# Turning the strips of the two output projections through tiles of the ring

## The chip, the cores and the metric

The kernel runs on one core of one Trainium2 chip. The metric is the device time of one execution in microseconds (us); lower is better. Times given for a kernel are medians over executions on the chip; the profile is one more execution, recorded by the hardware profiler.

## What is computed

The reference is a two-layer decoder trunk on 256 tokens of width 2048 in float32. Cut to what matters here:

```
for i in range(DEPTH):                                  # DEPTH = 2
    h = rms_norm(x, attn_norm_w[i])
    x = x + mixer(h, ...)                               # attention, then "@ w_o": the output projection
    x = x + conv_ffn(rms_norm(x, ffn_norm_w[i]), ffn_w_up[i], ..., ffn_w_down[i])
    gate = sigmoid(rms_norm(x, ple_norm_w[i]) @ ple_w_gate[i])
    x = x + gate * (p[i] @ ple_w_proj[i])
return rms_norm(x, final_norm_w)
```

The output projection multiplies the attention's result (256 x 2048 in layer 0, 256 x 1536 in layer 1) by `w_o` and adds the product to the stream x. The feed-forward part (FFN) then needs x, normalized, as the left operand of its up-projection.

## The kernel before

Every large product is made of float32 matmuls in a split form: each operand is a high part (`hi`, the value rounded to the matmul's type) and a low part (`lo`, the rest), and a block of 128 rows takes three matmuls for each half of the tokens (lines 360 to 362, `add_block`). ScalarE (ACT) makes `whi` of a raw weight tile (line 323) and VectorE (DVE) makes `wlo` (line 324); four pairs of `whi` and `wlo` exist (`NWSP = 4`), each holding two blocks of 128 rows, so that a pair is worth 12 matmuls of a strip. A product's output is made in strips of 512 columns, with tokens on the partitions, 128 tokens in each of two halves.

The next product wants x the other way round, with columns of x on the partitions. So each finished strip s of x is turned: DVE turns 32 x 32 squares of both halves into two tiles `y` (`turn_out`, line 248), a DMA on the queue of GpSimd (POOL) writes each `y` to a tile `there` in DRAM (line 251), and four DMAs read `there` back into a tile `turned` in the right order (`turn_in`, line 260). Then `use` makes four tiles `h` of it (`split_x`, lines 148 on ACT and 149 on DVE): the blocks 4s to 4s+3 of the next product's left operand. Below, h(s) stands for these four tiles of strip s, and y(s) for its two transposes.

`add_strips` runs a projection: for each of four strips it adds the product to x (line 983), squares it for the norm (line 216), and calls `Turned.add`, which first writes down the `use` of the strip ahead, h(s-1), and then the turning of strip s. The last strip's `use` is returned as `late` and is called by the next product. The calls to `add_strips` that make `h` are the output projection of each layer (`base` is 0) and the second half of each down-projection (`base` is not 0); the per-layer-embedding part (`ple`) has a `Turned` of its own.

The tiles `y` of these strips come from the pool `tmp`, under the tags `eh` and `el`, with one buffer each. The tiles `h`, the attention's results `o` and others come from the pool `ring`, with 42 buffers under one tag. The order of instructions on each engine is set ahead of time by a scheduler from the written order, the priorities, `issue_after`, and when tiles of a pool can be had; on the chip each engine then runs its list in order.

After the output projection the FFN takes its first two up-strips together (`products` with `side` 2 and `late`): both run over the blocks of h(0) to h(2), and then over those of h(3). In layer 1 the tiles are called `accv_12249` and `accv_12256` (the two halves of the gate strip), `accv_12353` and `accv_12360` (of the value strip), `h_11978` to `h_11987` for h(0), `h_12042` to `h_12051` for h(1), `h_12177` to `h_12186` for h(2) and `h_12461` to `h_12470` for h(3).

Of the kernel before, what the change touches and what calls it, by code (L numbers as in the profile page):

```python
# [80 lines left out]
def tile_trunk(ctx, tc, head_d, xT_d, x_d, pT_d, pos_d, vec_d, cst_d, csb_d, wqkv, wo_a, wkv, wq_b, wo_b, wup, wdn, wpg, wpp, gfin_d, out_d):  # L81
# [11 lines left out]
    def nm(s):  # L93
        uid[0] += 1
        return f"{s}_{uid[0]}"
# [7 lines left out]
    def rt(s, shape=(P, 512), dt=F32):  # L103
        return ring.tile(list(shape), dt, tag="kb", name=nm(s))

    def tt(s, shape=(P, S), dt=F32, tag=None, bufs=None):
        kw = {} if bufs is None else {"bufs": bufs}
        return tmp.tile(list(shape), dt, tag=tag or s, name=nm(s), **kw)
# [33 lines left out]
    def split_x(src, j, bases):  # L142

        out = []
        for b in bases:
            h = rt("h", dt=F32R)
            high, low = like(h[:, :S], src), like(h[:, S:], src)
            last["split"] = nc.scalar.activation(high, src, AF.Copy, scale=gain(b, j)).ins
            nc.vector.scalar_tensor_tensor(low, src, gain(b, j), f32(high), op0=OP.mult, op1=OP.subtract)
            out.append(h)  # L150
        return out
# [6 lines left out]
    def strip_of(t, s):  # L158
        return x[t][:, s * 512 : (s + 1) * 512]

    def load_table():

        table = nc.scalar.preload_act_table_set("natural_log_exp_and_others")
        tc.keep_in_program_order(table)
        return table
# [11 lines left out]
    class FirstNorm:  # L177


        def __init__(self):  # L180
            self.two = rt("first")
            self.s = self.two[:, :S]
            self.n = 0
            self.table = load_table()

        def add(self, src):

            if self.n == 0:
                nc.scalar.activation(self.two, src, AF.Square)
            else:  # L190
                q = tt("sq", (P, 768), tag="w", bufs=4)[:, :512]
                nc.scalar.activation(q, src, AF.Square)
                nc.vector.tensor_tensor(self.two, self.two, q, op=OP.add)
            self.n += 1
# [44 lines left out]
    def four(s):  # L239

        return tt(s, (P, 4 * S), tag="four", bufs=3)

    def turn_out(strips, ringed=False):

        there = dram.tile([2 * P, 512], F32, tag="turn", name=nm("there"))
        for t, strip in enumerate(strips):
            y = rt("y") if ringed else tt("y", (P, 768), tag=("eh", "el")[t], bufs=1)[:, :512]
            last["turned"] = nc.vector.transpose(  # L248
                y.rearrange("p (b o r) -> p o b r", b=4, o=4), strip.rearrange("p (o b c) -> p o b c", o=4, b=4)
            ).ins  # L250
            nc.gpsimd.dma_start(there[t * P : (t + 1) * P], y)  # L251
        return there

    def turn_in(there, ahead=0):

        z = four("turned").rearrange("p (a o r) -> p a o r", a=8, o=4)
        back = there.rearrange("(a c) (b f) -> b c a f", c=32, b=4)
        with tc.high_priority(offset=ahead) if ahead else ExitStack():
            for b in range(4):
                nc.gpsimd.dma_start(z[32 * b : 32 * b + 32].rearrange("p a o r -> p a (o r)"), back[b])  # L260
        return z

    def turn(s):
        z = turn_in(turn_out([strip_of(t, s) for t in range(2)]))
        return [z[:, :, o] for o in range(4)]

    class Turned:


        def __init__(self, use):  # L270
            self.use = use
            self.strip = None

        def add(self, s, later=False):
            if self.strip is not None:
                self.turn_strips(self.strip, later)
            self.strip = (s, turn(s))

        def turn_strips(self, strip, later):
            def use():  # L280
                with tc.issue_after(last["square"]), tc.issue_after(last["added"]):
                    self.use(*strip)

            self.waiting = use
            if not later:
                use()

        def late(self):
            self.use(*self.strip)

        def begin(self, tiles):
            return {4: self.waiting}

    def weights(W, s, n, fine=False, before=lambda k0: None, block=None, base=0, ringed=0):

# [81 lines left out]
    def products(jobs, xs, late=None, at=0, then={}, side=2, first=None, seven=None, plan=PLAN, host=lambda: None):  # L377
# [7 lines left out]
        if late is not None:  # L385
# [7 lines left out]
            def before(k0):  # L393
                if k0 + skip == at:
                    add()
                if k0 in then:
                    then[k0]()
# [24 lines left out]
            if at is None:  # L422
                W, s, base = jobs[0]
                ready = list(weights(W, s, 4, base=base + n))
                add()
# [36 lines left out]
    class Seven:  # L462
# [99 lines left out]
        def go_on(self):  # L562
            xs, n = self.xs[4:], len(self.xs) - 4
            ps = self.banks()[0]
            it = weights(self.W, self.strips[0], n, base=self.base + 4)

            def add(tiles, o):
                for k0, hi, lo in tiles:
                    for i in range(2):
                        add_block(ps[o], xs[k0 + i], o, hi[i], lo[i], False, k0 + i == n - 1, True)  # L570

            self.fifth()
            tiles = [next(it) for _ in range(2)]
            add(tiles, 0)
            self.sixth()
            add(tiles, 1)
            for k, o, hi, lo in (g for group in steps(hooked(it, {1: self.seventh}), n, 2) for g in group):
                add_block(ps[o], xs[k], o, hi, lo, False, k == n - 1, True)
            return ps
# [380 lines left out]
    def add_strips(W, xs, gain_of, norm, base=0, late=None, at=6, side=2, first=None, seven=None, plan=PLAN, host=None):  # L960

        out = []

        def use(s, blocks):
            for o, b in enumerate(blocks):
                out.extend(split_x(b, 4 * s + o, [gain_of]))

        turned = Turned(use)
        begun = [None]

        def hosted():
            if host is not None:
                begun[0] = host(out)
            if seven and norm is not None and not base:
                return turned
            return begun[0]

        jobs = [(W, s, base) for s in range(4)]
        for s, ps in enumerate(products(jobs, xs, late, at, {}, side, first, seven, plan, hosted)):
            if norm is not None and s == 3:  # L980
                norm.table = load_table()
            for t in range(2):
                last["added"] = nc.vector.tensor_tensor(strip_of(t, s), ps[t], strip_of(t, s), op=OP.add).ins
                if norm is not None:
                    norm.add(s, t)
            if norm is not None:
                turned.add(s, seven and not base and s == 2)
        return out, turned.late, begun[0]

    def ffn(i, xs, late, rc, began):  # L990
# [79 lines left out]
        def down_strips(gs, base, late, first, gain_of=None, norm=None):  # L1070
            if first:
                seven = Seven(wdn[i], 2, 3, gs, first.sums, base, ("acc", "two", "acc", "two"))
            else:
                seven = Seven(wdn[i], 2, 3, gs, block_sums(gs[:4]), base)
            return add_strips(wdn[i], gs, gain_of, norm, base, late, first=first, seven=seven)
# [93 lines left out]
    norm = FirstNorm()  # L1169
# [39 lines left out]
    for i in range(2):  # L1209
        norm = Norm()  # L1210
        seven = None
        host = lambda h: Seven(wup[i], 0, FB // 4, h, block_sums(h[:4]), 0, ("att", "acc", "acc", "acc"))
        h, late, began = add_strips(
            wo_a if i == 0 else wo_b,
            o,
            G_FFN + i * KB,
            norm,
            late=o_late,
            at=(10, 4)[i],
            side=2 + i,  # L1220
            seven=seven,
            plan=PLAN_WO,
            host=host if False else None,
        )
        rc = norm.done()
        pb = p_blocks(i)
        h, late, norm = ffn(i, h, late, rc, began)
        rc = norm.done()
        norm = Norm()
        if i == 0:  # L1230
            hq, xT, late = ple(i, h, late, pb, rc, norm, G_ATTN + KB)
            o, o_late = mixer_b(hq, late, lambda js: [split_x(xT[j], j, [G_KV])[0] for j in js], norm.done)
        else:
            ple(i, h, late, pb, rc, norm)
# [81 lines left out]
```

## Time and profile before

| | before |
|---|---|
| median of 3 runs | 2276.11 us (2276.03 to 2281.66) |
| the profiled execution's own time | 2277.94 us |
| its span in the trace | 2276.2 us |
| granted TensorE clock, mean | 0.999 |
| output projection of layer 0, last strip added to x | 374.5 us into the span |
| output projection of layer 1, last strip added to x | 1456.9 and 1460.5 us into the span |

The span is the trace from the first to the last instruction; 1.74 us of the execution's own time lie around it. The profiled execution is 1.83 us above the median of the runs. In the rows of a timeline the columns are: start, duration (both in us), engine, line, operation, output<-input, shape and count; in brackets the idle time of the engine ahead of the row and what ended it. A row with x2 or x4 merges neighbours.

### The profile page before, as it was taken

What the parts mean: (1) busy time and instruction counts of PE and PEld (TensorE: products, weight loads), DVE (VectorE), ACT (ScalarE), POOL (GpSimd) and SP (SyncE); (2) the same over time, 40 slices, a digit from 0 to 9 for tenths busy, and PEclk for the clock granted to TensorE, in tenths of its full rate; (3) what the DMA queues carried; (4) which work ended last, traced back from release to release, by engine and by line L of the source; (5) the groups of instructions that cost most, each with busy time, mean ns of one, the idle gap of its engine ahead of it and who ended that gap; (6) DMA issues with size and microseconds to landing.
All of it is one profiled execution on the core that took longest, in us unless ns stands there. A gap on an engine that the chain in (4) does not pass through costs nothing.

```text
span 2276.2 us, 28094 instructions
## 1 busy us (share of the span) xinstructions
PE 2262.8 (99%) x10095; PEld 1875.1 (82%) x10095; DVE 1720.8 (76%) x2532; ACT 1334.3 (59%) x1785; POOL 328.7 (14%) x575
## 2 busy tenths in 40 slices
PE   9999999999999999999999999999999999999998
PEld 7888888888888888888888888888888888888887
DVE  7778766788975888876787765768887588887665
ACT  6555555666644666655675554666664466665554
POOL 0211211111100111101021331211110011110100
PEclk9999999999999999999999999999999999999999
DMA  8678767686755867758587786868675577775863
GB/s 298 236 243 274 248 217 259 211 266 233 251 203 185 274 224 242 268 180 272 185 294 244 248 265 216 264 214 272 227 256 196 200 254 232 243 264 186 276 220 121
DMA packets 149549, 538.45 MB, mean 237 GB/s; under 512 B 16672, under 2 KB 17568, under 8 KB 149152
## 3 DMA queue, kind: packets, MB, share of 16 engines
q1 hardware_dynamic: 114560, 435.46, 55.0%
q0 software_dynamic: 32560, 95.98, 14.1%
q10 hardware_dynamic: 2288, 5.21, 0.7%
q8 instruction: 79, 1.29, 0.2%
q14 instruction: 62, 0.51, 0.1%
HBM read 486.52 MB, written 50.07 MB: 236 GB/s over the span
## 4 chain that ended last, share of the span: by engine, by line
PE 99%; DMA 1%; ACT 0%; DVE 0%; POOL 0%; issue 0%
PE accv L360 20%; PE accv L361 20%; PE accv L362 20%; PE seven L362 5%; PE seven L361 5%; PE seven L360 5%; PE seven L499 5%; PE two L362 4%; PE two L361 4%; PE two L360 4%; PE two L499 3%; PE two L626 1%; DMA turned<-there 0%; PE keys L626 0%; DMA vec<-in_head 0%; ACT whi L323 0%
## 5 line engine op out<-in xcount | busy, mean ns | idle before, releaser
L324 DVE TENSOR_TENSOR wlo<-raw,whi 128x1024 fp32r<-128x1024 f32 (+1 forms) x756 | 915.7, 1214 | 412.3 <-ACT whi L323 409.8
L323 ACT ACTIVATE whi<-raw 128x1024 fp32r<-128x1024 f32 (+1 forms) x756 | 794.8, 1053 | 654.6 <-PE accv L362 339.3
L360 PE MATMUL accv<-whi,h 128*128 128x512 f32 (+1 forms) x1496 | 580.9, 388 | 2.2 <-ACT whi L323 1.4
L362 PE MATMUL accv<-whi,h 128*128 128x512 f32 (+1 forms) x1496 | 580.8, 388 | 0.0
L361 PE MATMUL accv<-wlo,h 128*128 128x512 f32 (+1 forms) x1496 | 580.7, 388 | 0.0
L360 PEld LDWEIGHTS accv<-whi,h 128*128 128x128 f32 x1496 | 280.9, 188 | 60.7 <-ACT whi L323 2.0
L361 PEld LDWEIGHTS accv<-wlo,h 128*128 128x128 f32 x1496 | 280.9, 188 | 58.4 <-DVE wlo L324 0.7
L362 PEld LDWEIGHTS accv<-whi,h 128*128 128x128 f32 x1496 | 281.0, 188 | 57.4
L251 POOL DMA_DIRECT2D there<-y x162 | 91.7, 567 | 1265.4 <-DVE y L248 1245.5
L260 POOL DMA_DIRECT2D turned<-there x324 | 190.2, 594 | 453.7 <-DMA there<-y 195.6
L489 ACT ACTIVATE whi<-raw 128x1024 fp32r<-128x1024 f32 x119 | 126.0, 1059 | 103.5 <-PE accv L362 79.3
L490 DVE TENSOR_TENSOR wlo<-raw,whi 128x1024 fp32r<-128x1024 f32 x119 | 145.1, 1219 | 44.1 <-ACT whi L489 43.5
L362 PE MATMUL seven<-whi,h 128*128 128x512 f32 x384 | 150.0, 391 | 0.0
L361 PE MATMUL seven<-wlo,h 128*128 128x512 f32 x384 | 149.4, 389 | 0.0
L360 PE MATMUL seven<-whi,h 128*128 128x512 f32 x384 | 149.4, 389 | 0.0
L360 PE MATMUL accv<-whi,g 128*128 128x512 f32 x352 | 136.9, 389 | 0.0
L361 PE MATMUL accv<-wlo,g 128*128 128x512 f32 x352 | 136.9, 389 | 0.0
L362 PE MATMUL accv<-whi,g 128*128 128x512 f32 x352 | 136.9, 389 | 0.0
L360 PE MATMUL two<-whi,h 128*128 128x512 f32 x240 | 93.4, 389 | 0.0
L361 PE MATMUL two<-wlo,h 128*128 128x512 f32 x240 | 93.4, 389 | 0.0
L362 PE MATMUL two<-whi,h 128*128 128x512 f32 x240 | 93.4, 389 | 0.0
L248 DVE STREAM_TRANSPOSE y<-u 128x512 f32<-128x512 f32 x122 | 84.0, 699 | 5.0 <-DMA there<-y 4.6
(230 smaller groups left out, 3214.7 us busy)
## 6 DMA issues: line engine op xcount, KB each, us to landing
raw<-in_wup SPq DMA_DIRECT2D x176, 1024.0 KB, 5.5
raw<-in_wdn SPq DMA_DIRECT2D x88, 1024.0 KB, 5.4
there<-y POOLq DMA_DIRECT2D x171, 256.0 KB, 5.1
turned<-there POOLq DMA_DIRECT2D x324, 128.0 KB, 5.1
raw<-in_wqkv SPq DMA_DIRECT2D x40, 1024.0 KB, 5.5
raw<-in_wpg SPq DMA_DIRECT2D x32, 1024.0 KB, 5.5
raw<-in_wkv SPq DMA_DIRECT2D x24, 1024.0 KB, 5.5
raw<-in_wo_a SPq DMA_DIRECT2D x16, 1024.0 KB, 5.9
```

The lines of the kernel that those rows point to most:

```text
L248: last["turned"] = nc.vector.transpose(y.rearrange("p (b o r) -> p o b r", b=4, o=4), strip.rearrange("p (o b c) -> p o b c", o=4, b=4)).ins
L251: nc.gpsimd.dma_start(there[t * P : (t + 1) * P], y)
L260: nc.gpsimd.dma_start(z[32 * b : 32 * b + 32].rearrange("p a o r -> p a (o r)"), back[b])
L323: last["high"] = nc.scalar.activation(hi[:, c], r, AF.Copy).ins
L324: last["low weights"] = nc.vector.tensor_tensor(lo[:, c], r, f32(hi[:, c]), op=OP.subtract).ins
L360: nc.tensor.matmul(ps, xl, hi, start=first, stop=False, skip_group_check=again)
L361: nc.tensor.matmul(ps, xh, lo, start=False, stop=False, skip_group_check=again)
L362: nc.tensor.matmul(ps, xh, hi, start=False, stop=final, skip_group_check=again)
L489: last["high"] = nc.scalar.activation(hi, r, AF.Copy).ins
L490: last["low weights"] = nc.vector.tensor_tensor(lo, r, f32(hi), op=OP.subtract).ins
L499: nc.tensor.matmul(ps, x, y, start=begins, stop=ends, skip_group_check=True)
L626: run.append(nc.tensor.matmul(*args, skip_group_check=True, **kw).ins)
```

## The change

`turn` and `Turned` get an argument `ringed`, which reaches `turn_out`: with it the two `y` of a strip are tiles of the ring, and not the two single tiles of the tags `eh` and `el`. `add_strips` sets it where `base` is 0, so for both output projections: 4 strips x 2 halves x 2 layers, 16 tiles. The down-projections and `ple` keep the single tiles. The other lines removed belong to a delayed call of `use` (`later`, `turn_strips`, `begin`) whose condition holds in no call of this kernel: `seven` with `norm` and without `base` occurs nowhere.

```
-    def turn(s):
-        z = turn_in(turn_out([strip_of(t, s) for t in range(2)]))
+    def turn(s, ringed=False):
+        z = turn_in(turn_out([strip_of(t, s) for t in range(2)], ringed))
         return [z[:, :, o] for o in range(4)]
 
     class Turned:
-        def __init__(self, use):
+        def __init__(self, use, ringed=False):
             self.use = use
             self.strip = None
-
-        def add(self, s, later=False):
+            self.ringed = ringed
+
+        def add(self, s):
             if self.strip is not None:
-                self.turn_strips(self.strip, later)
-            self.strip = (s, turn(s))
...
                 with tc.issue_after(last["square"]), tc.issue_after(last["added"]):
-                    self.use(*strip)
...
+                    self.use(*self.strip)
+            self.strip = (s, turn(s, self.ringed))
...
-        turned = Turned(use)
+        turned = Turned(use, not base)
...
-            if seven and norm is not None and not base:
-                return turned
...
-                turned.add(s, seven and not base and s == 2)
+                turned.add(s)
```

The numbers and kinds of instructions stay the same on every engine; the order changes on PE, DVE and ACT, around the two output projections only. POOL and the queue of SP keep theirs. Line numbers after the class fall by 10 to 12 (324 becomes 314, 983 becomes 971).

On DVE, output projection of layer 1, strip 1 (its sums are `x_76<-accv_11741` and `x_77<-accv_11748`, its transposes `y_11991` and `y_11994`). Before:

```order
L983 TENSOR_TENSOR x_76<-accv_11741,x_76 128x512
L983 TENSOR_TENSOR x_77<-accv_11748,x_77 128x512
L248 STREAM_TRANSPOSE y_11991<-x_76 128x4x4x32
L324 TENSOR_TENSOR wlo_12087<-raw_12066,whi_12086 128x1024
L248 STREAM_TRANSPOSE y_11994<-x_77 128x4x4x32
L324 TENSOR_TENSOR wlo_12105<-raw_12102,whi_12104 128x1024
L983 TENSOR_TENSOR x_76<-two_11805,x_76 128x512
L983 TENSOR_TENSOR x_77<-two_11805,x_77 128x512
L324 TENSOR_TENSOR wlo_12121<-raw_12102,whi_12120 128x1024
L324 TENSOR_TENSOR wlo_12139<-raw_12136,whi_12138 128x1024
L149 SCALAR_TENSOR_TENSOR h_11978<-turned_11933,vec,h_11978 128x256
```

The same place on DVE with the change:

```order
L971 TENSOR_TENSOR x_76<-two_11805,x_76 128x512
L971 TENSOR_TENSOR x_77<-two_11805,x_77 128x512
L314 TENSOR_TENSOR wlo_12121<-raw_12102,whi_12120 128x1024
L314 TENSOR_TENSOR wlo_12139<-raw_12136,whi_12138 128x1024
L149 SCALAR_TENSOR_TENSOR h_11978<-turned_11933,vec,h_11978 128x256
L149 SCALAR_TENSOR_TENSOR h_11981<-turned_11933,vec,h_11981 128x256
L149 SCALAR_TENSOR_TENSOR h_11984<-turned_11933,vec,h_11984 128x256
L149 SCALAR_TENSOR_TENSOR h_11987<-turned_11933,vec,h_11987 128x256
L248 STREAM_TRANSPOSE y_11991<-x_76 128x4x4x32
L314 TENSOR_TENSOR wlo_12155<-raw_12136,whi_12154 128x1024
L248 STREAM_TRANSPOSE y_11994<-x_77 128x4x4x32
```

The transposes y(1) moved from right behind strip 1's sums to behind the four h(0), where y(2) stood before.

On DVE, the same projection, strip 3 (`y_12190`, `y_12193`) and h(2). Before:

```order
L983 TENSOR_TENSOR x_77<-accv_12079,x_77 128x512
L248 STREAM_TRANSPOSE y_12190<-x_76 128x4x4x32
L248 STREAM_TRANSPOSE y_12193<-x_77 128x4x4x32
L324 TENSOR_TENSOR wlo_12316<-raw_12313,whi_12315 128x1024
L235 TENSOR_REDUCE rcol_12201<-ssum_11664 128x2
L169 TENSOR_SCALAR rcol_12201<-rcol_12201 128x2
L324 TENSOR_TENSOR wlo_12332<-raw_12313,whi_12331 128x1024
L149 SCALAR_TENSOR_TENSOR h_12177<-turned_12061,vec,h_12177 128x256
L149 SCALAR_TENSOR_TENSOR h_12180<-turned_12061,vec,h_12180 128x256
L149 SCALAR_TENSOR_TENSOR h_12183<-turned_12061,vec,h_12183 128x256
L149 SCALAR_TENSOR_TENSOR h_12186<-turned_12061,vec,h_12186 128x256
```

With the change:

```order
L314 TENSOR_TENSOR wlo_12420<-raw_12417,whi_12419 128x1024
L149 SCALAR_TENSOR_TENSOR h_12177<-turned_12061,vec,h_12177 128x256
L149 SCALAR_TENSOR_TENSOR h_12180<-turned_12061,vec,h_12180 128x256
L149 SCALAR_TENSOR_TENSOR h_12183<-turned_12061,vec,h_12183 128x256
L149 SCALAR_TENSOR_TENSOR h_12186<-turned_12061,vec,h_12186 128x256
L248 STREAM_TRANSPOSE y_12190<-x_76 128x4x4x32
L314 TENSOR_TENSOR wlo_12436<-raw_12417,whi_12435 128x1024
L248 STREAM_TRANSPOSE y_12193<-x_77 128x4x4x32
```

The transposes y(3), which stood ahead of h(2), now stand behind it; between h(1) and h(2) y(2) moved in the same way, and in layer 0 all three.

On PE, where the FFN of layer 1 has used up h(1) (`h_12051` is its last tile). Before:

```order
L360 MATMUL accv_12256<-whi_12297,h_12051 128x512
L361 MATMUL accv_12256<-wlo_12298,h_12051 128x512
L362 MATMUL accv_12256<-whi_12297,h_12051 128x512
L360 MATMUL accv_12249<-whi_12315,h_12177 128x512
L361 MATMUL accv_12249<-wlo_12316,h_12177 128x512
L362 MATMUL accv_12249<-whi_12315,h_12177 128x512
```

With the change:

```order
L350 MATMUL accv_12256<-whi_12297,h_12051 128x512
L351 MATMUL accv_12256<-wlo_12298,h_12051 128x512
L352 MATMUL accv_12256<-whi_12297,h_12051 128x512
L350 MATMUL accv_12353<-whi_12349,h_11978 128x512
L351 MATMUL accv_12353<-wlo_12350,h_11978 128x512
L352 MATMUL accv_12353<-whi_12349,h_11978 128x512
```

Here 48 matmuls of the value strip over h(0) and h(1) moved ahead of the gate strip's 24 over h(2). In layer 0 PE keeps its order.

More of the change, by code (lines that the diff above doesn't have):

```diff
@@ L261, in turn_in @@
         return z
-    def turn(s):
-        z = turn_in(turn_out([strip_of(t, s) for t in range(2)]))
+    def turn(s, ringed=False):
+        z = turn_in(turn_out([strip_of(t, s) for t in range(2)], ringed))
         return [z[:, :, o] for o in range(4)]
     class Turned:
-        def __init__(self, use):
+        def __init__(self, use, ringed=False):
             self.use = use
             self.strip = None
-        def add(self, s, later=False):
+            self.ringed = ringed
+        def add(self, s):
             if self.strip is not None:
-                self.turn_strips(self.strip, later)
-            self.strip = (s, turn(s))
-        def turn_strips(self, strip, later):
-            def use():
                 with tc.issue_after(last["square"]), tc.issue_after(last["added"]):
-                    self.use(*strip)
-            self.waiting = use
-            if not later:
-                use()
+                    self.use(*self.strip)
+            self.strip = (s, turn(s, self.ringed))
         def late(self):
             self.use(*self.strip)
-        def begin(self, tiles):
-            return {4: self.waiting}
     def weights(W, s, n, fine=False, before=lambda k0: None, block=None, base=0, ringed=0):
```

## The prediction

> **What bounds the kernel now.** I read the page's table of engines first, then the chain of waits of TensorE (PE), then the same stretch engine by engine.
>
> ```profile
> span 2276.2 us, 28094 instructions
> PE 2262.8 (99%) x10095; PEld 1875.1 (82%) x10095; DVE 1720.8 (76%) x2532; ACT 1334.3 (59%) x1785; POOL 328.7 (14%) x575
> ```
>
> PE is busy all but 13.4 us of the span, so the time is that of its list of matmuls plus its idle time. Its waits on other engines:
>
> ```profile
> PE accv L360 <- ACT whi L323: 1.4, 1, 1.4
> PE warm L130 <- DVE zero L127: 1.2, 1, 1.2
> PE accv L360 <- DVE h L149: 0.9, 1, 0.9
> ```
>
> The first two are the program's start. The third is the only wait in the middle, and it is the change's place: the FFN of layer 1 waits for h(2). PE's rows around it, with the first matmul on an h:
>
> ```profile
> 1457.78 0.39 PE L360 MATMUL accv<-whi,h 128*128 128x512 f32 x1
> ...
> 1468.43 0.39 PE L362 MATMUL accv<-whi,h 128*128 128x512 f32 x1
> 1469.67 0.50 PE L360 MATMUL accv<-whi,h 128*128 128x512 f32 x1 [0.85 <-DVE h L149]
> ```
>
> The second row is the 48th matmul: (1468.43 - 1457.78) / 47 = 0.2266 us each. So 24 matmuls, one h(s) in one up-strip, are worth 5.44 us, and a pair of weights 2.72 us. Without a wait h(2) would have begun at 1468.66, so PE lost 1.0 us. That is about all that the change can win on PE; anything else it can only lose.
>
> **What the old tiles cost, and what stands in its place.** DVE in that stretch:
>
> ```profile
> 1436.93 0.70 DVE L248 STREAM_TRANSPOSE y<-x 128x512 f32<-128x512 f32 x1
> ...
> 1439.61 0.71 DVE L248 STREAM_TRANSPOSE y<-x 128x512 f32<-128x512 f32 x1 [0.87 <-DMA there<-y]
> ...
> 1446.90 1.69 DVE L149 SCALAR_TENSOR_TENSOR h<-turned,vec,h 128x256 fp32r<-128x256 f32 x4 [0.21 <-ACT h L148]
> 1448.51 0.70 DVE L248 STREAM_TRANSPOSE y<-x 128x512 f32<-128x512 f32 x1
> ...
> 1450.24 0.70 DVE L248 STREAM_TRANSPOSE y<-x 128x512 f32<-128x512 f32 x1
> ...
> 1461.11 1.30 DVE L248 STREAM_TRANSPOSE y<-x 128x512 f32<-128x512 f32 x2
> ```
>
> y(1) waited 0.87 us for the buffer `el`, on an engine with slack; removing that wait is worth nothing by itself. But look at when the transposes ran: y(1) at 1436.93, y(2) at 1448.51, y(3) at 1461.11, each as soon as sums and buffers allowed, so that several strips were on their way through DRAM together. In the new order of DVE y(s) stands behind all four h(s-1), and h(s-1) waits for the read-back of strip s-1. A ring gives its tiles in written order, in which `use` of strip s-1 comes first; that is how I read the order, but only the order itself enters the sum. On an engine that runs its list in order, three strips that overlapped become a serial chain: y(1), trip through DRAM, h(1), y(2), trip, h(2), y(3), trip, h(3).
>
> **One trip, from rows.** POOL (writes L251, read-backs L260) and ACT's first step on what landed:
>
> ```profile
> 1434.22 0.56 POOL L251 DMA_DIRECT2D there<-y  x1 [1.15 <-DVE y L248]
> 1440.07 2.35 POOL L260 DMA_DIRECT2D turned<-there  x4 [5.29 <-ACT whi L323]
> 1442.41 1.12 POOL L251 DMA_DIRECT2D there<-y  x2
> 1448.00 2.35 POOL L260 DMA_DIRECT2D turned<-there  x4 [4.46 <-ACT h L148]
> ...
> 1451.23 0.56 POOL L251 DMA_DIRECT2D there<-y  x1 [0.32 <-DVE y L248]
> 1459.41 2.35 POOL L260 DMA_DIRECT2D turned<-there  x4 [7.62 <-ACT whi L323]
> 1462.11 1.15 POOL L251 DMA_DIRECT2D there<-y  x2 [0.35 <-DVE y L248]
> 1470.20 2.35 POOL L260 DMA_DIRECT2D turned<-there  x4 [6.94 <-ACT h L148]
> ```
>
> ```profile
> 1446.36 1.71 ACT L148 ACTIVATE h<-turned,vec 128x256 fp32r<-128x256 f32 x4 [0.92 <-DMA turned<-there]
> ...
> 1455.08 0.91 ACT L148 ACTIVATE h<-turned,vec 128x256 fp32r<-128x256 f32 x2 [1.48 <-DMA turned<-there]
> ...
> 1468.59 0.51 ACT L148 ACTIVATE h<-turned,vec 128x256 fp32r<-128x256 f32 x1 [3.79 <-DMA turned<-there]
> ```
>
> Layer 0, the same steps of strip 0:
>
> ```profile
> 329.55 0.56 POOL L251 DMA_DIRECT2D there<-y  x1 [1.16 <-DVE y L248]
> 336.11 2.35 POOL L260 DMA_DIRECT2D turned<-there  x4 [6.00 <-issue]
> ```
>
> ```profile
> 343.64 1.71 ACT L148 ACTIVATE h<-turned,vec 128x256 fp32r<-128x256 f32 x4 [2.92 <-DMA turned<-there]
> 344.19 1.69 DVE L149 SCALAR_TENSOR_TENSOR h<-turned,vec,h 128x256 fp32r<-128x256 f32 x4 [2.20 <-ACT h L148]
> ```
>
> - a, from the first transpose to the second write's issue: 1451.23 - 1448.51 = 2.72 us (a weight split runs between the two transposes, and the new order keeps one there).
> - b, from that issue to the first read-back's: 5.85, 5.0 (the second write of 1442.41 starts at 1442.97), 8.18, 7.5 and, in layer 0, 6.56. Mean 6.6.
> - c, from the first read-back's issue to ACT's h, where ACT waited for the landing: 6.29, 7.08, 9.18 and, in layer 0, 7.53. Mean 7.5.
> - d, from ACT's h to the end of the four on DVE: 1446.90 + 1.69 - 1446.36 = 2.23. From ACT's h to PE's first matmul on it: 1469.67 - 1468.59 = 1.08.
>
> A full trip is T = a + b + c + d = 19.05 us; to ACT's h it is 16.82.
>
> **Layer 1, the term that decides.** y(1) takes the place that y(2) had, 1448.51.
> - h(1): ACT 1448.51 + 16.82 = 1465.33, PE 1466.41. PE needs it at 1457.78 + 5.44 = 1463.22: waits 3.2 us. h(1) ends on DVE at 1467.56, where y(2) starts.
> - h(2): ACT 1484.38, PE 1485.46. In the new order PE first has h(1) in the gate strip and h(0), h(1) in the value strip, 3 x 5.44 = 16.32 us, so needs h(2) at 1482.73: waits 2.7. y(3) starts at 1486.61.
> - h(3): ACT 1503.43, PE 1504.51. Until then PE has only h(2) in two strips, 10.88 us, to 1496.34: waits 8.2.
>
> Before, PE came to h(3) at 1469.67 + 5.44 + 3 x 5.44 = 1491.43. The matmuls ahead of that point are the same, so the loss is 1504.51 - 1491.43 = 13.1 us; the old wait of 1.0 is in it. As a formula, with h(3) on PE at 1448.51 + 3T - 1.15: loss = 3T - 44.07. The value strip's turn ahead is PE's cover, and it hides 10.88 us of the second trip; the third has no such cover.
>
> **Layer 0, hidden by little.** There PE starts the FFN later against its turning:
>
> ```profile
> 374.83 0.39 PE L360 MATMUL accv<-whi,h 128*128 128x512 f32 x1
> ```
>
> h(0) ends at 344.19 + 1.69 = 345.88, where y(1) starts. h(1) reaches ACT at 362.70; h(2), from y(2) at 364.93, reaches ACT at 381.75 and PE at 382.8, needed at 374.83 + 10.88 = 385.7. A weight split now stands between its halves, 1.2 us, so y(3) starts at 385.2; h(3) is at PE at 403.1, needed at 374.83 + 6 x 5.44 = 407.5. No wait for an h, with 2.9 us to spare. Tighter is what queues behind h(1) on ACT and DVE, the weights of the projection's sixth pair:
>
> ```profile
> L324 DVE TENSOR_TENSOR wlo<-raw,whi 128x1024 fp32r<-128x1024 f32 (+1 forms) x756 | 915.7, 1214 | 412.3 <-ACT whi L323 409.8
> L323 ACT ACTIVATE whi<-raw 128x1024 fp32r<-128x1024 f32 (+1 forms) x756 | 794.8, 1053 | 654.6 <-PE accv L362 339.3
> ```
>
> ACT ends h(1) at 364.4 and `whi` at 365.5; DVE ends h(1) at 364.9, a transpose at 365.6, `wlo` at 366.8. PE wants that `wlo` at 374.83 - 3 x 2.72 + 0.23 = 366.9. I take 0, with 0.1 us in hand. In layer 1 such weights don't bind: while PE waits for an h, the pairs ahead are ready.
>
> **The rest costs nothing.** The kinds and counts of instructions, POOL's list and SP's list stay, so no DMA is added and none moves past another in its queue. Ring tiles as `y` add no wait at the transposes in the new order but DVE's own. The removed branches never ran.
>
> **Sum.** 13.1 us on the profiled execution's span of 2276.2: 2289.3. Its own time of 2277.94 is 1.83 above the runs' median of 2276.11, so the forecast for the median is 2276.1 + 13.1 = 2289.
>
> **Bounds.** The fastest write in this trace with one read-back behind it:
>
> ```profile
> 1642.87 0.56 POOL L251 DMA_DIRECT2D there<-y  x1 [3.48 <-DVE y L248]
> 1646.89 1.21 POOL L260 DMA_DIRECT2D turned<-there  x2 [3.47 <-ACT whi L323]
> ```
>
> With b = 4.0 and c = 6.29, T is 15.2. Then PE no longer waits for h(1) or h(2), but ACT's list has a `whi` ahead of h(2) that needs a pair which PE frees at 1468.66 + 3 x 2.72 = 1476.82 (two of the four pairs are held for h(2)): ACT takes h(2) at 1478.0, y(3) starts at 1480.2, h(3) is on PE at 1494.3, a loss of 2.9 us: 2279. With all trips at b = 8.18 and c = 9.18, T is 22.3, the loss 22.8, and in layer 0 the weights behind h(1) and h(2) come 3 us late each: 2305. Trips vary separately, so three at one end are unlikely; I take 2281 to 2300.
>
> **Rivals.**
> - Not slower: short trips. PE that waits frees no weight buffers, SP's loads stop, and the trips have the DMA engines to themselves, toward b = 4.0 and c = 6.3. For it: write gaps of 4 us exist. Against: ACT waited 3.79 us for a landing while PE stood, and that trip took 9.18. By the formula the loss is under 6.8 us (0.3%, about what a measurement of this kernel tells from no change) when T is below 17.0. Time 2279. Chance 0.13.
> - The cold clock. A long wait of PE may cost its clock afterwards:
>
> ```profile
> 1465.00:1470.00 5.00, 4.15 (x18) 3.11 (x17) 1.61 (x4) 1.41 (x4) 0.00 (x0) 1.00 0.97 332
> 2265.00:2276.00 11.00, 1.23 (x11) 0.78 0.29 96
> ```
>
> The granted clock (the third column from the end) stayed 1.00 over the short wait; it was 0.78 in the tail, where PE was busy for 1.23 of 11 us. If a wait of 8 us acts like the tail, 11 x 0.22 = 2.4 us come on top: 2291.5. The wait of 8.2 is nearer to the tail than to 0.85, but that clock was read while PE had hardly anything to do. Chance 0.20. [...]
> - Layer 0 waits too. Its margin of 0.1 us goes if h(1) lands late; at the slow end it costs 6 us: about 2295. Chance 0.11.
> - A gain: trips overlap as before in spite of the order, and the 1.0 us wait goes: 2275. Against it: DVE runs its list in order. Chance 0.02; a gain of over 0.3% has no source, since PE's only wait there is 1.0.
>
> **Chances.** The sum as worked out, 0.54. Slower by over 0.3%: 0.54 + 0.20 + 0.11 = 0.85; within 0.3%: 0.13 + 0.02 = 0.15, of which I leave 0.01 to a gain over 0.3% whose source I don't see: 0.14 and 0.01.
>
> **What would show it.** Right: in layer 1 DVE's y(1) to y(3) each right behind an h, about 19 us apart; PE waits on h three times, growing to about 8 us; POOL's write-to-read gaps as before; layer 0 with no wait over 1 us. Wrong: trips of under 17 us, or PE waiting in layer 0 on `wlo`, or a granted clock below 1 after 1500.

## The result, and the profile after

The changed kernel takes 2289.07 us, the median of 8 runs (2287.0 to 2301.02), against 2276.75 us for the kernel before (8 runs, 2276.03 to 2281.66): slower by 12.3 us, 0.54% by the medians. The ratio on record, which is formed over all the runs and not as the quotient of the two medians, is 1.006, with a 95% interval of 1.0048 to 1.0072. The profiled execution of the changed kernel took 2287.04 us with a span of 2285.3, against 2277.94 and 2276.2 before: 9.1 us, and that is the difference that the two traces can explain.

The head of the page and the table of engines, after:

```profile
span 2285.3 us, 28077 instructions
PE 2265.1 (99%) x10095; PEld 1875.3 (82%) x10095; DVE 1721.7 (75%) x2532; ACT 1335.2 (58%) x1785; POOL 327.7 (14%) x575
```

The counts of matmuls and of DVE's instructions are those of before. PE idles for 20.2 us where it idled for 13.4, and it is busy for 2.3 us longer with the same 10095 matmuls. So there are two losses, not one: TensorE stands longer, and some of its matmuls run more slowly. TensorE's waits, after (total, times, longest):

```profile
PE accv L350 <- DVE h L149: 8.0, 4, 5.6
PE warm L130 <- DVE zero L127: 1.2, 1, 1.2
PE accv L351 <- DVE wlo L314: 1.1, 2, 0.9
```

One of the four waits on `h`, 1.2 us, belongs to the program's start, where the kernel before waited for a `whi`. The other three are in the FFN of layer 1. PE's rows there, from the first matmul on an h:

```profile
1458.83 0.39 PE L350 MATMUL accv<-whi,h 128*128 128x512 f32 x1
...
1465.34 0.50 PE L350 MATMUL accv<-whi,h 128*128 128x512 f32 x1 [0.91 <-DVE h L149]
...
1482.34 0.50 PE L350 MATMUL accv<-whi,h 128*128 128x512 f32 x1 [0.34 <-DVE h L149]
...
1499.11 0.80 PE L350 MATMUL accv<-whi,h 128*128 128x512 f32 x1 [5.55 <-DVE h L149]
1499.70 0.63 PE L351 MATMUL accv<-wlo,h 128*128 128x512 f32 x1
1500.13 0.63 PE L352 MATMUL accv<-whi,h 128*128 128x512 f32 x1
...
1502.26 0.42 PE L351 MATMUL accv<-wlo,h 128*128 128x512 f32 x1
1502.52 0.40 PE L352 MATMUL accv<-whi,h 128*128 128x512 f32 x1
```

PE waits for h(1) 0.91 us, for h(2) 0.34, for h(3) 5.55. Behind the long wait the matmuls start 0.43 us apart until 1502.26, and soon after at the usual 0.2266. DVE in the same stretch:

```profile
1449.42 0.70 DVE L248 STREAM_TRANSPOSE y<-x 128x512 f32<-128x512 f32 x1
...
1464.80 1.68 DVE L149 SCALAR_TENSOR_TENSOR h<-turned,vec,h 128x256 fp32r<-128x256 f32 x4 [0.73 <-ACT h L148]
1466.40 0.70 DVE L248 STREAM_TRANSPOSE y<-x 128x512 f32<-128x512 f32 x1
...
1481.80 1.68 DVE L149 SCALAR_TENSOR_TENSOR h<-turned,vec,h 128x256 fp32r<-128x256 f32 x4 [0.17 <-ACT h L148]
1483.40 0.70 DVE L248 STREAM_TRANSPOSE y<-x 128x512 f32<-128x512 f32 x1
...
1498.57 1.68 DVE L149 SCALAR_TENSOR_TENSOR h<-turned,vec,h 128x256 fp32r<-128x256 f32 x4 [2.66 <-ACT h L148]
```

Each transpose stands right behind the four h of the strip ahead: y(1) at 1449.42, y(2) at 1466.40, y(3) at 1483.40. The serial chain is there, with trips of 16.98 and 17.00 us. The second writes, the read-backs and ACT's first step on the landed strip, for the same three trips, first POOL and then ACT:

```profile
1452.14 0.56 POOL L251 DMA_DIRECT2D there<-y  x1 [1.16 <-DVE y L248]
1459.17 2.34 POOL L260 DMA_DIRECT2D turned<-there  x4 [6.47 <-DMA there<-y]
...
1469.18 0.56 POOL L251 DMA_DIRECT2D there<-y  x1 [1.21 <-DVE n L174]
1474.89 2.34 POOL L260 DMA_DIRECT2D turned<-there  x4 [5.15 <-DMA there<-y]
...
1486.13 0.56 POOL L251 DMA_DIRECT2D there<-y  x1 [1.15 <-DVE y L248]
1492.15 2.34 POOL L260 DMA_DIRECT2D turned<-there  x4 [5.47 <-ACT whi L313]
```

```profile
1464.26 1.71 ACT L148 ACTIVATE h<-turned,vec 128x256 fp32r<-128x256 f32 x4 [1.45 <-DMA turned<-there]
...
1481.26 0.91 ACT L148 ACTIVATE h<-turned,vec 128x256 fp32r<-128x256 f32 x2 [0.89 <-DMA turned<-there]
...
1498.03 1.70 ACT L148 ACTIVATE h<-turned,vec 128x256 fp32r<-128x256 f32 x4 [3.38 <-DMA turned<-there]
```

By these, b (from the second write's issue to the first read-back's) was 7.03, 5.71 and 6.02 us, and c (from there to ACT's h) was 5.09, 6.37 and 5.88. The clock, in windows of the changed kernel (time, length, busy time of PE, PEld, DVE, ACT and POOL, granted clock, share of the DMA engines, GB/s):

```profile
330.00:400.00 70.00, 70.00 (x311) 57.95 (x310) 48.79 (x71) 39.22 (x57) 12.75 (x22) 1.00 0.78 254
...
1495.00:1500.00 5.00, 0.89 (x2) 0.80 (x3) 2.34 (x5) 1.70 (x4) 0.00 (x0) 0.89 0.94 284
1500.00:1505.00 5.00, 5.00 (x18) 3.96 (x18) 0.53 (x2) 1.07 (x2) 0.00 (x0) 0.77 0.04 15
1505.00:1510.00 5.00, 5.00 (x23) 4.13 (x22) 3.42 (x4) 3.25 (x4) 0.99 (x2) 1.00 0.23 59
```

The first row lies in layer 0, where PE is busy throughout, and PE has no wait at all between 300 and 420 us: nothing was lost there. The granted clock falls to 0.77 in the window in which the slow matmuls lie, and is back at 1.00 after it.

The accounting needs the moment at which PE came to h(3) in the kernel before, the 145th matmul from 1457.78 on:

```profile
1491.60 0.39 PE L360 MATMUL accv<-whi,h 128*128 128x512 f32 x1
```

The prediction worked out 1491.43 for it; the 0.17 between them is what PE's restart behind its short wait cost (1469.67 to 1470.01 is 0.34 us, and the next matmuls too are a little over 0.2266 apart). Behind this row 2276.2 - 1491.60 = 784.60 us were left. After the change PE came to h(3) at 1499.11, with 2285.3 - 1499.11 = 786.19 left. So 7.51 us were lost ahead of h(3) and 1.59 behind it: together the 9.1. Of the 7.51, 1.05 were there at the first matmul on an h (1458.83 against 1457.78); they are a wait of 0.9 us on a `wlo` at 452 us, far from the two projections, with its restart. The trace of the same kernel in experiment 9 lacks that wait. That leaves 6.46 for the chain. Of the 1.59, 0.17 are again a restart, as experiment 7 shows, and 1.42 the slow matmuls.

### The profile page after: what moved, and what is told of

It is laid out like the page before. It is cut to its first block, busy times and chain, and to the rows that moved or that the text cites. A ratio compares the mean times of both kernels' runs of the same rounds, so it can differ in the third digit from the quotient of the medians.

```text
span 2285.3 us, 28077 instructions
## 1 busy us (share of the span) xinstructions
PE 2265.1 (99%) x10095; PEld 1875.3 (82%) x10095; DVE 1721.7 (75%) x2532; ACT 1335.2 (58%) x1785; POOL 327.7 (14%) x575
## 4 chain that ended last, share of the span: by engine, by line
PE 95%; DMA 2%; DVE 1%; ACT 0%; issue 0%; POOL 0%; SPq 0%; DVEq 0%; POOLq 0%; ACTq 0%
PE accv L350 19%; PE accv L351 19%; PE accv L352 19%; PE seven L351 5%; PE seven L350 5%; PE seven L352 5%; PE seven L489 5%; PE two L350 4%; PE two L351 4%; PE two L352 4%; PE two L489 2%; PE two L616 1%; DMA there<-y 1%; DMA turned<-there 1%; DVE wlo L314 0%
```

## Experiments

In the diffs below a minus or plus is against the changed kernel, unless the text says otherwise. Times are medians, each beside the median of runs of the kernel before on the same chip; the ratios are formed as above.

| | kernel | median, us | runs of the kernel before, us | ratio, 95% interval |
|---|---|---|---|---|
| 1 | layer 0 only | 2278.64 | 2277.65 | 1.0000, 0.9990 to 1.0009 |
| 2 | layer 1 only | 2286.53 | 2277.65 | 1.0037, 1.0025 to 1.0050 |
| 3 | ring tiles, order of before | 2277.99 | 2277.65 | 1.0003, 0.9994 to 1.0011 |
| 4 | old tiles, serial order | 2285.41 | 2277.65 | 1.0034, 1.0021 to 1.0046 |
| 5 | ring tiles for strip 3 only | 2276.60 | 2277.38 | 1.0000, 0.9992 to 1.0009 |
| 6 | ring tiles for strips 2 and 3 | 2282.42 | 2277.38 | 1.0026, 1.0015 to 1.0036 |
| 7 | changed kernel with PE kept at work | 2284.38 | 2277.38 | 1.0038, 1.0026 to 1.0051 |
| 8 | two strips turned ahead | 2276.72 | 2277.38 | 1.0001, 0.9992 to 1.0010 |
| 9 | changed kernel again | 2285.93 | 2276.97 | 1.0045, 1.0029 to 1.0060 |
| 10 | layer 1 only, again | 2285.84 | 2276.97 | 1.0034, 1.0021 to 1.0047 |
| 11 | PE kept at work, again | 2285.29 | 2276.97 | 1.0041, 1.0025 to 1.0057 |

Seven of these medians lie outside the range that was expected by the theory that they are then read to support. Experiments 1, 3, 6 and 8 came out 0.6, 1.0, 0.4 and 0.2 us above it, and experiments 2, 4 and 7 came out 0.5, 1.6 and 1.1 below. The medians of the kernel before themselves lie between 2276.75 and 2277.65, so the readings below go by the runs beside each experiment and by the traces.

### Which layer: experiments 1, 2, 9 and 10

The change is applied to one layer's projection at a time (`side` is 2 in layer 0's call and 3 in layer 1's).

```
-        turned = Turned(use, not base)
+        turned = Turned(use, not base and side == 2)     # experiment 1
+        turned = Turned(use, side == 3)                  # experiments 2 and 10
```

> Ring tiles and the new order in layer 0 alone. Serial-chain theory: layer 0 has cover for all three trips, so 2276 to 2278 us and no wait of PE on an h near 375 to 410 us. Rival (layer 0 pays as well, through weights that queue behind h on ACT and DVE): 2279 to 2282.

> Ring tiles and the new order in layer 1 alone. Serial-chain theory: the whole loss is here, 2287 to 2291 us, with three waits of PE on h between 1460 and 1505 us, the last the longest (5 to 8 us). Rival (layer 0 pays as well): 2283 to 2285.

> The changed kernel once more, beside the next two on one chip. If layer 0 costs nothing, it comes out as the kernel with layer 1 alone, 2285 to 2288 us (ratio 1.0035 to 1.005), and the 1.006 of the first measurement held long trips of that occasion. Rival (the two layers add up): 2 to 4 us above the kernel with layer 1 alone.

> Ring tiles in layer 1 alone, again: 2285 to 2288 us; the same as the changed kernel beside it if layer 0 costs nothing, 2 to 4 us under it if the layers add up.

Layer 0 alone gives no difference that the ratio shows, layer 1 alone all of it: on one chip the whole change took 2285.93 us and layer 1 alone 2285.84. By its median of 2278.64 alone experiment 1 would lie between its two ranges; what settles it is its ratio, the pair of experiments 9 and 10, and its trace, in which PE has no wait between 14 and 1440 us. The wait on h(2) in layer 1 stands there as it did before the change, 1.83 us against 0.85, and in the trace of experiment 2 the long wait is the one of the changed kernel:

```profile
1470.55 0.50 PE L350 MATMUL accv<-whi,h 128*128 128x512 f32 x1 [1.83 <-DVE h L149]
```

```profile
1497.20 0.79 PE L350 MATMUL accv<-whi,h 128*128 128x512 f32 x1 [5.60 <-DVE h L149]
```

### Tiles or order: experiments 3 and 4

The change does two things at once: `y` comes from the ring, and on DVE it stands behind the h ahead. These two experiments do one without the other. Experiment 3 keeps the ring's tiles and writes the turning of a strip ahead of `use` of the strip before:

```
         def add(self, s):
-            if self.strip is not None:
+            ahead, ringed = self.strip, self.ringed
+            if ringed:
+                self.strip = (s, turn(s, ringed))
+            if ahead is not None:
                 with tc.issue_after(last["square"]), tc.issue_after(last["added"]):
-                    self.use(*self.strip)
-            self.strip = (s, turn(s, self.ringed))
+                    self.use(*ahead)
+            if not ringed:
+                self.strip = (s, turn(s))
```

Experiment 4 is the kernel before (the diff is against it), with its two single tiles, and only puts the transposes behind the last h of the strip ahead:

```
-            nc.vector.scalar_tensor_tensor(low, src, gain(b, j), f32(high), ...)
+            last["h"] = nc.vector.scalar_tensor_tensor(low, src, gain(b, j), f32(high), ...).ins
...
-    def turn(s):
-        z = turn_in(turn_out([strip_of(t, s) for t in range(2)]))
+    def turn(s, behind=False):
+        with tc.issue_after(last["h"]) if behind else ExitStack():
+            there = turn_out([strip_of(t, s) for t in range(2)])
+        z = turn_in(there)
...
-            self.strip = (s, turn(s))
+            self.strip = (s, turn(s, self.behind and self.strip is not None))
```

> Ring tiles as in the change, but strip s is turned in the written order ahead of h(s-1), which puts the transposes back on DVE where they were before. Serial-chain theory: 2275.5 to 2277 us, as before, with one PE wait on h of 0 to 1 us. Rival (the ring's tiles themselves cost, by waits for buffers or where they lie): 2286 to 2291.

> The two old single tiles, but the transposes of strip s are ordered behind h(s-1), as in the change; the order of DVE, ACT and PE around the projections is then nearly that of the change. Serial-chain theory: 2287 to 2291 us with the same three waits. Rival (the ring's tiles themselves cost): 2276 to 2278.

Experiment 3 is as fast as the kernel before; experiment 4 is slower, nearly by what the change in layer 1 alone costs on the same chip (2285.41 against 2286.53). DVE's transposes y(1), y(2) and y(3) of layer 1, first in experiment 3 and then in experiment 4:

```profile
1436.53 0.70 DVE L248 STREAM_TRANSPOSE y<-x 128x512 f32<-128x512 f32 x1
...
1447.96 0.71 DVE L248 STREAM_TRANSPOSE y<-x 128x512 f32<-128x512 f32 x1
...
1462.79 1.29 DVE L248 STREAM_TRANSPOSE y<-x 128x512 f32<-128x512 f32 x2
```

```profile
1448.94 0.70 DVE L248 STREAM_TRANSPOSE y<-x 128x512 f32<-128x512 f32 x1
...
1465.52 0.70 DVE L248 STREAM_TRANSPOSE y<-x 128x512 f32<-128x512 f32 x1
...
1482.23 1.30 DVE L248 STREAM_TRANSPOSE y<-x 128x512 f32<-128x512 f32 x2
```

With ring tiles and the old order y(3) runs at 1462.79, as it did at 1461.11 before; with the old tiles in the serial order it runs at 1482.23. The time goes with the order; the tiles themselves cost and bring nothing that can be measured. PE waits 4.52 us for h(3) in experiment 4, about 1 us less than with the change; there the two transposes y(3) run back to back (the x2 of the row), and the last trip is shorter by about as much. The wait for `el` that the change takes away is gone in experiment 3 too (y(1) follows its own first half in 1.73 us), and nothing is faster for it.

### How much of the chain: experiments 5 and 6

Ring tiles for some of the strips, so that the chain has one link or two (strips 0 and 1 never get one here):

```
-            self.strip = (s, turn(s, self.ringed))
+            self.strip = (s, turn(s, self.ringed and s == 3))     # experiment 5
+            self.strip = (s, turn(s, self.ringed and s >= 2))     # experiment 6
```

> Ring tiles for the last strip of each projection alone: one serial trip, behind h(2). Serial-chain theory: y(3) starts near 1471 us in layer 1, h(3) reaches PE 16 to 18 us later, at 1487 to 1489, ahead of the 1491.4 at which PE needs it: 2276 to 2277.5 us. Rival (each move costs its share, a third of the loss): 2280 to 2281.

> Ring tiles for strips 2 and 3: two serial trips. Serial-chain theory: y(2) starts near 1460.5 us, h(2) is on PE near 1477 with a wait of 2 to 4 us, h(3) near 1495 against 1491.4 before: 2279 to 2282 us. Rival (two thirds of the loss): 2284 to 2286; rival (only the number of ring tiles counts, half of them): 2283.

One link costs nothing: y(3) runs at 1468.12, ACT starts on h(3) at 1485.39, and PE comes to it only at 1489.66, without a wait:

```profile
1489.66 0.39 PE L350 MATMUL accv<-whi,h 128*128 128x512 f32 x1
```

Two links cost 5 to 6 us, with y(2) at 1459.56, where DVE is done with h(1), and y(3) at 1477.23, behind h(2). PE and the clock in experiment 6 (ring tiles for strips 2 and 3):

```profile
1476.18 0.50 PE L350 MATMUL accv<-whi,h 128*128 128x512 f32 x1 [2.41 <-DVE h L149]
...
1477.44 0.44 PE L352 MATMUL accv<-whi,h 128*128 128x512 f32 x1
1477.68 0.63 PE L350 MATMUL accv<-whi,h 128*128 128x512 f32 x1
...
1481.08 0.39 PE L352 MATMUL accv<-whi,h 128*128 128x512 f32 x1
...
1495.39 0.50 PE L350 MATMUL accv<-whi,h 128*128 128x512 f32 x1 [1.20 <-DVE h L149]
```

PE waits for h(2) and a second time for h(3). The matmuls lose speed here too: the 9 from 1477.44 to 1481.08 take 3.64 us instead of 2.04, and those 1.6 us are not in any wait.

### The cold clock: experiments 7 and 11

The changed kernel with 22 more matmuls in layer 1, between the last on h(2) and the first on h(3), into a bank that nothing reads. They fill some 5 us of PE's wait with work whose result is thrown away. The rival to a cold clock is that the slow matmuls come from what they read.

```
+                calls[0] += 1
+                if calls[0] == 4:
+                    ps = bank("fill")
+                    for i in range(22):
+                        nc.tensor.matmul(ps, xs[n - 1][:, :P], xs[n - 1], start=True, stop=True, ...)
```

> The changed kernel with 22 matmuls more in layer 1, between PE's last matmul on h(2) and its first on h(3), on an h(2) tile and into a bank that nobody reads (about 5 us of work inside the wait of 5 to 8 us). Cold-clock theory: the granted clock stays 1.00 after the wait, the first eight matmuls on h(3) are 0.23 us apart, not 0.43, and 1.6 us come back: 2285.5 to 2289 us, 1 to 2 under the changed kernel. Rival (the slow matmuls come from what they read, not from the clock): no change, 2287 to 2291, or longer where the wait is under 5 us.

> The changed kernel with the 22 filling matmuls, again: by the cold clock 1 to 2 us under the changed kernel beside it, 2283.5 to 2287 us; by the rival the same as it. In its profile the first matmuls on h(3) are 0.23 us apart where the wait behind the filling is under 2 us.

PE in experiment 7 around h(3):

```profile
1499.13 5.15 PE L420 MATMUL fill<-h 128*128 128x512 f32 x22
1505.04 0.50 PE L351 MATMUL accv<-whi,h 128*128 128x512 f32 x1 [0.76 <-DVE h L150]
...
1507.02 0.39 PE L353 MATMUL accv<-whi,h 128*128 128x512 f32 x1
```

The last row is the ninth matmul on h(3): 8 of them took 1.98 us, against 3.41 in the changed kernel (1499.11 to 1502.52) and 8 x 0.2266 = 1.81 without any wait. From the first matmul on h(3) to the end, experiment 7 has 2289.8 - 1505.04 = 784.76 us and experiment 11 2288.3 - 1503.55 = 784.75, where the kernel before, which has no wait there, has 784.60 and the changed one 786.19. The 0.16 between the first two and the third are what a restart costs anyway (1.98 - 1.81 = 0.17). So the other 1.42 us behind h(3) come from PE's having stood idle, and matmuls in the gap take them away, though the matmuls on h(3) read the same tiles as before. The granted clock stays 1.00 from 1495 to 1510 us in experiment 7. This is read from the traces. The times alone do not settle it: in the one set that has both, 2285.29 us with the filler and 2285.93 without, 0.6 apart, within the scatter of either (2283.62 to 2295.07, and 2284.59 to 2296.19). The profiled execution of experiment 7 was its longest, 2291.56 us, with a wait of 5.6 us at 83 us, near the program's start, that is no part of this.

The filler also delivered an accident. In experiment 11 DVE's y(1), y(2) and y(3), and PE at h(1), read:

```profile
1448.30 0.71 DVE L249 STREAM_TRANSPOSE y<-x 128x512 f32<-128x512 f32 x1
...
1468.35 0.70 DVE L249 STREAM_TRANSPOSE y<-x 128x512 f32<-128x512 f32 x1
...
1487.74 0.70 DVE L249 STREAM_TRANSPOSE y<-x 128x512 f32<-128x512 f32 x1
```

```profile
1467.29 0.70 PE L351 MATMUL accv<-whi,h 128*128 128x512 f32 x1 [3.96 <-DVE h L150]
1467.79 0.63 PE L352 MATMUL accv<-wlo,h 128*128 128x512 f32 x1
```

Trips of 20.05 and 19.39 us, where experiment 7, the same kernel, has 16.55 and 16.69. So the trip's length is a matter of the execution, and the forecast's 19.05 is inside what occurs. The longer trips differ in the transfers: b was 7.46 and 5.70 us against 5.87 and 5.85 in experiment 7, and c 7.72 and 8.76 against 5.81 and 5.71. It was not that the DMA engines were busier: over the two read-backs c they were 77 and 83% busy, against 91 and 92% in experiment 7. All profiled executions with the three serial trips, from rows of the same kind as above:

| | y(1) to y(2), us | y(2) to y(3), us | first matmul on h(3) | from there to the end, us | slow matmuls cost, us |
|---|---|---|---|---|---|
| changed kernel | 16.98 | 17.00 | 1499.11 | 786.19 | 1.43 |
| changed kernel again | 16.98 | 16.74 | 1497.77 | 786.23 | 1.49 |
| layer 1 only | 16.74 | 16.71 | 1497.20 | 786.60 | 1.82 |
| layer 1 only, again | 16.89 | 16.80 | 1496.84 | 787.46 | 2.72 |
| old tiles, serial order | 16.58 | 16.71 | 1496.87 | 786.73 | 1.94 |
| PE kept at work | 16.55 | 16.69 | 1505.04 | 784.76 | 0 |
| PE kept at work, again | 20.05 | 19.39 | 1503.55 | 784.75 | 0 |

The last column is the time from the first matmul on h(3) to the first at full speed, less 0.2266 for each in it, less the 0.17 that a restart costs anyway (1.98 - 1.81, above). It accounts for the column before it to within 0.1 us: 784.60 + 0.17 + 1.43 = 786.20, and 784.60 + 0.17 + 2.72 = 787.49.

### More overlap: experiment 8

If overlap of trips is what counts, more of it may take away the old wait of 1.0 us. Strips 0 to 2 are turned before any h is written, strip 3 ahead of h(2):

```
+            if self.ringed:
+                self.strips.append((s, turn(s, True)))
+                with tc.issue_after(last["square"]), tc.issue_after(last["added"]):
+                    for strip in {2: [0, 1], 3: [2]}.get(s, []):
+                        self.use(*self.strips[strip])
+                self.strip = self.strips[-1]
+                return
```

> Ring tiles, and the strips 0 to 2 are turned ahead of any h in the written order, strip 3 ahead of h(2): more trips overlap than before. Serial-chain theory: h(2) is there before PE needs it, the wait of 1.0 us of the kernel before goes too, 2275 to 2276.5 us. Rival (crowding: more transfers in flight make each trip longer and h(1) late): 2277 to 2281.

It takes what the kernel before takes. PE's waits in it, and its first matmuls on h(0) and h(3) in layer 1:

```profile
PE accv L359 <- DVE wlo L322: 1.5, 3, 0.9
...
PE seven L359 <- DVE wlo L322: 0.8, 1, 0.8
PE accv L358 <- DVE h L149: 0.4, 1, 0.4
```

```profile
1460.21 0.39 PE L358 MATMUL accv<-whi,h 128*128 128x512 f32 x1
...
1492.85 0.39 PE L358 MATMUL accv<-whi,h 128*128 128x512 f32 x1
```

The wait on h(2) is gone: between the two rows lie 144 matmuls in 32.64 us, without any wait, where the kernel before took 33.82 (1457.78 to 1491.60). So the stretch itself gains 1.2 us. The waits on `wlo`, 2.3 us in all, lie elsewhere, at 8, 444, 452 and 1177 us, and the 0.4 on `h` at 5 us. One of 0.9 at 452 us is in the changed kernel's trace too, so whether they come from this order is not shown. Experiment 5 takes the same 1.2 us less in the stretch (1457.03 to 1489.66), and its median shows no gain either. No version was found that beats the kernel before measurably; experiments 3, 5 and 8 equal it.

## Why the prediction was right, and where its sum was not

The forecast of 2289 us met the median of 2289.07. That it did so to a tenth of a microsecond is luck: two of its sizes were off, in opposite directions, and the same kernel took 2285.93 us in experiment 9. Two of the signs that the prediction itself had named as wrong came: a trip of under 17 us (16.98), and a granted clock below 1 after 1500 (0.77).

- **The place and the mechanism were right.** The loss is in layer 1, it comes from DVE's order and not from the tiles (experiments 3 and 4), and it is the serial chain y(1), trip, h(1), y(2), trip, h(2), y(3), trip, h(3), as DVE's rows show. PE waits three times and longest for h(3), though the waits did not grow from the first on.
- **The term T was sized too long for the profiled execution.** T = 19.05 was forecast; the two trips measured were 16.98 and 17.00, and in five more of the seven executions in the table 16.55 to 16.98. Of its parts a (2.72) and d (1.68 + 1464.80 - 1464.26 = 2.22, against 2.23) held, b came to 6.25 on average against 6.6, and c to 5.78 against 7.5: c is the part that was mis-sized. It came as a mean of four rows, of which one was 9.18. With T = 17.0 the prediction's own formula, 3T - 44.07, gives 6.9; the trace has 6.46, and the 0.17 by which 1491.43 was too early is part of the difference. All three waits shrank with it, from 3.2, 2.7 and 8.2 to 0.91, 0.34 and 5.55.
- **The cold clock, a rival given 0.20, came true on top.** It was priced at 2.4 us from the granted clock in the program's tail; it cost 1.43 to 2.72 in the five executions that waited long (1.43 in the profiled pair). In these five the slow matmuls start 0.43 us apart, against 0.2266 at full speed, and the slow stretch lasts 3.4 to 6.1 us after the restart. The waits on an h of 2.4 us and more in these traces, seven from 2.41 to 5.67 us, were all followed by slow matmuls, so for the 8.2 us forecast the sum should have held them.
- **Together they make 6.46 + 1.59, restart and slow matmuls, and 9.1 with the 1.05 of an earlier wait**, where the sum had 13.1. That the medians nevertheless lie 12.3 us apart has two parts: the profiled execution of the kernel before was 1.2 us above its median, and that of the changed one (2287.04, close to the lowest of 2287.0 to 2301.02) 2.0 below. Trips of 19 to 20 us do occur and would give it: in experiment 11 PE came to h(3) 45.82 - 33.82 = 12.0 us later, counted from its first matmul on an h, than in the kernel before. But no long execution of the changed kernel itself was traced, so that this is the reason is inferred. The later set of the same kernel has 2285.93, nearer to what the trace explains.
- **The rival of short trips** named T below 17.0 as the point where the loss sinks under 0.3%. T came to about that point, and the loss stayed above it only with the cold clock added. It was a closer thing than 0.13 said. The reason that it gave, trips that have the DMA engines to themselves, is not what the traces show: over the six stretches b and c in the changed kernel the engines were 81 to 89% busy, against 76 to 99% in the four of strips 0 and 2 before. Why the trips were shorter is not shown: read-backs of overlapping strips (c in the kernel before 6.29, 7.08, 9.18; in experiments 3 and 5 from 5.85 to 9.19) and of serial ones (5.09 to 8.76) scatter over nearly the same range.
- **Layer 0 waits too** was wrong: PE was busy for 70.00 of the 70 us from 330 to 400, and experiments 1, 9 and 10 show no cost. The margin of 0.1 us was as thin as said, though: in experiment 4 PE waits 0.7 us in the projection of layer 0, at 367.4, on the kind of tile that was named, a `wlo`. **A gain** was wrong too: no trip overlapped.
- **The removed lines and the ring's tiles** cost nothing, as forecast: experiment 3 has both.

## What to carry to other kernels

A tile's tag can be what sets an engine's order: giving a step other buffers let it slip behind work that waits for a transfer, and three transfers that overlapped became three in a row. Before a buffer wait is taken away, look at what the waiting step is ahead of; here the wait was on an engine with slack, and its place in the order was worth ten times as much. A wait of TensorE can cost more than its length: behind the waits of 4.5 to 5.7 us here the matmuls started 0.43 us apart instead of 0.2266 for 3.4 to 6.1 us, and that cost 1.4 to 2.7 us more.

## What the hardware showed that was not expected

- The clock fell after shorter waits than the 8.2 us for which the prediction weighed it, and not always at once. After 5.55 us (the changed kernel) and 3.96 us (experiment 11) of idle time PE restarted slow, with matmuls 0.43 us apart; the granted clock was 0.77 from 1500 to 1505 us in the one and 0.74 from 1465 to 1470 us in the other. After 2.41 us (experiment 6) it restarted at full speed (0.23 us apart), fell to half speed (0.43) 1.5 us later, and stayed there for 3.4 us; the granted clock was 0.76 from 1475 to 1480 us. After 1.83 us (experiment 1) and 1.18 us (experiment 11) nothing happened: the granted clock stayed 1.00. What, beside the wait, makes the clock fall is not shown.
- How long the slow stretch lasts differs between executions with nearly the same wait: 3.4 us after 5.55 us idle, 6.1 us (1496.84 to 1502.90) after 5.67.
- One trip through DRAM of the same size, with the same instructions, took from 16.6 to 20.1 us. The longer ones took longer in their transfers (c was 7.72 and 8.76 us in experiment 11, against 5.81 and 5.71 in experiment 7), with the DMA engines no busier (77 and 83% over these, against 91 and 92%); what the transfers wait for was not found.
